# Value products of two head pairs in one group, up products grouped by operand, first loads by single row blocks, last update in unequal pieces

## The chip, the cores and the metric

The kernel runs on one core of one Trainium2 chip. A core has a matrix engine (TensorE, "PE" in the profile, with its weight loads under "PEld"), VectorE (DVE), ScalarE (ACT), GpSimd (POOL, all but unused here) and SyncE (SP), whose queue issues every transfer of this kernel. PE reads its operands from on-chip memory (SBUF) and writes into an accumulator memory (PSUM); ACT and DVE carry results out of it. The metric is the time of one execution in device microseconds, and the median over runs is compared.

## The reference, cut to what matters

Two layers of a decoder over 256 tokens of width 1024, in float32. Each layer has eight heads of sparse attention (three branches: compressed, selected, window), eight heads of forgetting attention, an output projection, and a squared-ReLU MLP, each wrapped in norms:

```python
for l in range(DEPTH):                       # DEPTH = 2
    h = _rms_norm(x, g_pre_mix[l])
    parts = jnp.split(h @ w_in[l], split_at, axis=-1)      # 1024 -> 2848 columns
    ...
    o_nsa = _nsa_mixer(...)                  # 8 heads of 64, branches gated by a sigmoid
    o_fox = _fox_mixer(...)                  # 8 heads of 64, decayed causal softmax
    mix = jnp.concatenate([o_nsa, o_fox], axis=-1) @ w_out[l]
    x = x + _rms_norm(mix, g_post_mix[l])
    h = _rms_norm(x, g_pre_mlp[l])
    y = jnp.square(jax.nn.relu(h @ w_up[l])) @ w_down[l]   # 1024 -> 4096 -> 1024
    x = x + _rms_norm(y, g_post_mlp[l])
```

With 256 tokens, selection keeps all four blocks and the window reaches over all tokens, so the selected and the window branch are both causal softmax attention over the whole sequence, each with its own keys and values.

## The kernel before, in words

**Arithmetic.** A float32 product is made of three products in a faster float32 form: each operand is split into a high part (an ACT copy, `whi` for weights) and a low remainder (a DVE subtraction, `wlo`), and the three products high-high, high-low and low-high are summed in PSUM (`mm3`). So each weight unit passes three steps: a transfer from memory into a raw buffer (`wraw`, four buffers, `RBUFS`), the ACT copy, and the DVE subtraction, after which the raw buffer is free. Attention probabilities, transposes and value products are plain float32.

**Order.** Nothing is issued in the order of the program text. A recorder (`Recorder`) collects all operations, then plays them through a planner with assumed costs and due times (`order`, line 243) and writes out one fixed order per engine. Each engine then runs its list in order, waiting on semaphores where operands are late. A `stretch` (line 182) binds several PE products into one piece of the plan; the planner charges 145 ns (`RETILE`) when the shape of the PE array that a product uses changes.

**Start.** `FIRSTS` (line 41) cuts the first 512-column chunk of the input projection by row blocks of 128: units of 1, 1, 2, 2 and 2 blocks. Lines 537 to 546 issue, on SP, the head (gains and row block 0 of x transposed), then weight units and blocks of x transposed (`xt`) in turns. Behind them come x itself in four pieces, constants, and the units of the next chunk. For the first units the split is done block by block (line 442).

**Attention.** Steps run over a flat list: for the sparse heads, pairs 0 to 3, two heads a pair, branches 1 and 2; then the forgetting heads, pairs 0 to 3, two heads. A step computes scores; one step later the probabilities are scaled; two steps later `probs_T` (line 1141) transposes them on PE (three transposes of 128x128) and copies them to SBUF as `prT`; three steps later, when a pair is complete, `pv` (line 1152) makes the value products of the pair in a stretch: 64-column weights, the two heads side by side, 8 products for a sparse pair and 4 for a forgetting pair, each run in two passes. A sparse pair adds one 128-column product with `vbig` for the compressed branch. `o_evac` (line 1167) splits the 256 columns of the result into high and low parts (`oT`). Between these steps PE is filled with products of the input projection and later of the output projection (`fill`). PSUM holds one accumulator of the kind "o".

**Output projection, MLP.** `out_last` (line 1283) finishes the output projection with blocks 4 to 7, which need the forgetting heads. In `up` (line 1319) the transposed up projection has weights stationary and tokens moving: for each of 28 column blocks of 128 a layer, and each of eight row blocks, one product of the high weights with 512 moving columns (high and low tokens side by side) and one of the low weights with 256. `down` products have 512 moving columns.

**End.** `sandwich` (line 656) applies the last norm and adds the result into x, in halves of 512 columns for each of the two token tiles, and stores each half.

Of the kernel before, what the change touches and what calls it, by code (L numbers as in the profile page):

```python
# [18 lines left out]
F32 = mybir.dt.float32  # L19
F32R = mybir.dt.float32r  # L20
AF = mybir.ActivationFunctionType
OP = mybir.AluOpType
PSUM = bass.MemoryType.PSUM

P = 128
# [12 lines left out]
RETILE = 145  # L38
SEQ = [(2, 0), (2, 1), (2, 2), (2, 3), (3, 0), (3, 1), (3, 2), (3, 3)]
EVKEY = 1  # L40
FIRSTS = [(0, 1), (1, 2), (2, 4), (4, 6), (6, 8)]
UPK = 7
TOK, WBUFS, RBUFS = 6, 7, 4
LOAD_LEAD, SPLIT_LEAD, RIDE_LEAD = 12, 1, 6
# [366 lines left out]
class Weights:  # L411
# [12 lines left out]
    def get(self, i):  # L424
        nc, marks = self.nc, self.marks
        assert len(marks) == i
        marks.append(len(nc.ops))
        if i not in self.raw:
            nc.key = marks[max(i - LOAD_LEAD, 0)]
            if self.units[i][0] == "raw":  # L430
                nc.after = nc.ops[marks[max(i - RIDE_LEAD, 0)] - 1]
            self.load(i)
            nc.after = None
        kind, shape, src = self.units[i]
        raw = self.raw.pop(i)
        nc.key = None
        if kind == "raw":
            return raw
        nc.key = marks[max(i - SPLIT_LEAD, 0)]
        hi = self.tile([P] + shape, F32R, name="whi", tag="whi", bufs=WBUFS)  # L440
        lo = self.tile([P] + shape, F32R, name="wlo", tag="wlo", bufs=WBUFS)
        for j in range(shape[0]) if i < len(FIRSTS) else [slice(None)]:
            nc.scalar.activation(hi[:, j], raw[:, j], AF.Copy)
            nc.vector.tensor_sub(lo[:, j], raw[:, j], hi[:, j].bitcast(F32))
        nc.key = None
        return hi, lo
# [14 lines left out]
def trunk(nc, A, consts_in, out, sbp, pp):  # L461
# [75 lines left out]

    nc.sync.dma_start(head, A["xT"][:, 0:8 + S])
    W.load(0)
    load_xt(1, 3)  # L540
    W.load(1)
    W.load(2)
    load_xt(3, 5)
    W.load(3)
    load_xt(5, 8)
    W.load(4)
    nc.after = nc.ops[-1]

    def load_rest():
# [106 lines left out]
    def sandwich(t, acc, g_post, pre=None, xT=None, r4=None, r2=None, store=None):  # L656


        sq = small([P, 2], "sq")
        m, mg = [None, None], [None, None]  # L660

        def times(name, n, gain):
            y = tokt(name)
            if r2 is None:
                nc.vector.tensor_mul(y, acc[n], gain[:, half(n)])
            else:
                nc.vector.scalar_tensor_tensor(y, acc[n], r2, gain[:, half(n)], op0=OP.mult, op1=OP.mult)
            return y

        for n in range(2):  # L670
            junk = small([P, 512], "rl")
            nc.scalar.activation(junk, acc[n], AF.Square, scale=1.0 / 32.0, accum_out=sq[:, n:n + 1])
            if pre:
                mg[n] = times("mg", n, pre[0])
            if n == 0 and not pre:
                m[0] = times("m", 0, g_post)
        r = rsqrt_sum(sq[:, 0:1], sq[:, 1:2], r4)
        if not pre:
            m[1] = times("m", 1, g_post)
        if pre:  # L680
            xg = []
            for n in range(2):
                xg.append(mg[n])
                for c in (0, 256):
                    a = n * 512 + c
                    nc.vector.scalar_tensor_tensor(xg[n][:, c:c + 256], mg[n][:, c:c + 256], r,
                                                   pre[1][t][:, a:a + 256], op0=OP.mult, op1=OP.add)
            yield
            for n in range(2):
                to_xT(t, n, xg[n], xT)  # L690
            yield
        for n in range(2):
            if pre:
                m[n] = times("m", n, g_post)
            nc.vector.scalar_tensor_tensor(X[t][:, half(n)], m[n], r, X[t][:, half(n)],
                                           op0=OP.mult, op1=OP.add)
            if store is not None:
                nc.sync.dma_start(store[:, half(n)], X[t][:, half(n)])
        yield

    def rope(dst, src, t, nh):
# [28 lines left out]
    for l in range(DEPTH):  # L730
# [407 lines left out]
                    nc.vector.tensor_scalar(p[:, a:b], p[:, a:b], st[:, 2 + t:3 + t], gate[t][:, c:c + 1],  # L1138
                                            op0=OP.mult, op1=OP.mult)

        def probs_T(p, eng):
            ps = psum("s")
            for a in (0, 128, 256):
                nc.tensor.transpose(ps[:, a:a + P], p[:, a:a + P], ident)
            pT = small([P, 384], "prT", 6)
            if eng:
                nc.scalar.activation(pT, ps[:, :384], AF.Copy)
            else:
                nc.vector.tensor_copy(pT, ps[:, :384])
            return pT  # L1150

        def pv(o, terms, last):

            with nc.stretch():
                for i, (pT, V, cols) in enumerate(terms):
                    for kb in range(2):
                        for par in range(2):
                            h = slice(par * HD, par * HD + HD)
                            c = cols[par]
                            if kb == 0:  # L1160
                                nc.tensor.matmul(o[h, 0:S], V[0][:, c:c + HD], pT[par][:, 0:S],
                                                 start=i == 0, stop=False, skip_group_check=True)
                            else:
                                nc.tensor.matmul(o[h, P:S], V[1][:, c:c + HD], pT[par][:, S:S + P],
                                                 start=False, stop=last and i == len(terms) - 1, skip_group_check=True)

        def o_evac(o, kind, pair):
            if (kind, 0) not in oT:
                for j in range(2):
                    oT[kind, j] = tile([P, 4, S], F32R, name="oT", tag=f"act{j}", bufs=2)  # L1170
            split(o[:, :S], [oT[kind, j][:, pair, :] for j in range(2)])
            done.add(("o", pair + (0 if kind == "nsa" else 4)))


        if first:
# [70 lines left out]
        for i in range(len(flat) + 4):  # L1246
            if 0 <= i - 1 < len(flat):
                scale(flat[i - 1], *st[i - 1])
            if i < len(flat):
                st[i] = scores(flat[i])  # L1250
                if i == 15:
                    done.add("nsa")
                    g_post, g_pre2 = load_gains(("g_post_mix", l), ("g_pre_mlp", l))
            fill(1)
            if i in side:
                side[i]()
                fill(1)
            if 0 <= i - 2 < len(flat):
                pTs[flat[i - 2]] = probs_T(st.pop(i - 2)[0], i % 2)
            fill(1)  # L1260
            j = i - 3
            if 0 <= j < len(flat) and flat[j][2] == 1 and flat[j][3] != 1:
                kind, pair, par, br = flat[j]
                o = psum("o")
                cols = [(pair // 2) * HD] * 2 if br else [2 * pair * HD, 2 * pair * HD + HD]
                pv(o, [([pTs.pop((kind, pair, x, b)) for x in range(2)], (fV, vS, vW)[b], cols)
                       for b in ((1, 2) if br else (0,))], not br)
                if br:
                    nc.tensor.matmul(o[:, :S], T["vbig"][:, pair].rearrange("p j d -> p (j d)"), T["pcT"],
                                     start=False, stop=True, skip_group_check=True)  # L1270
                o_evac(o, kind, pair)
            if i >= 12 or i % 2:
                fill(1)

# [44 lines left out]
        def up(fc, then=None):  # L1319
            a = [tile([P, 4, S], F32R, name="aT", tag=f"act{j}", bufs=2) for j in range(2)]  # L1320
            for b in range(4):
                hi, lo = weight(l, "up", fc, b)

                ps = psum("s")
                for k in range(8):
                    nc.tensor.matmul(ps, hi[:, k, :], xT[2][:, k].rearrange("p j n -> p (j n)"), start=k == 0, stop=False,
                                     skip_group_check=True)
                    nc.tensor.matmul(ps[:, S:], lo[:, k, :], xT[0][:, k, :], start=False, stop=k == 7,
                                     skip_group_check=True)
                if then is not None and b == 1:  # L1330
                    then()
                if b % 2 == 0:
                    h = tokt("h")
                d = h[:, (b % 2) * S:(b % 2) * S + S]
                nc.scalar.activation(d, ps[:, S:], AF.Copy)
                nc.vector.tensor_add(d, ps[:, :S], d)
                if b % 2:
                    rl = small([P, 512], "rl")
                    nc.scalar.activation(rl, h, AF.Relu)
                    nc.vector.tensor_mul(h, rl, rl)  # L1340
                    d = [y[:, b - 1:b + 1, :].rearrange("p b n -> p (b n)") for y in a]
                    nc.scalar.activation(d[0], rl, AF.Square)
                    nc.vector.tensor_sub(d[1], h, d[0].bitcast(F32))
# [122 lines left out]
```

## Time and profile before

| what | value |
|---|---|
| median of 3 runs | 635.33 us (635.32 to 635.46) |
| the profiled execution | 635.77 us, span 634.0 us |
| PE busy | 625.5 us, 99% of the span |
| ACT, DVE busy | 373.8 us, 480.9 us |
| DMA | 115.75 MB, mean 183 GB/s |

A row of a timeline gives start, duration, engine, line (L350 is the one line through which the recorder emits everything), operation, output and inputs by tile name, the array shape, the output's shape, and a count where rows are merged. Matmuls are pipelined, so a row's duration overlaps the next; what one costs is the distance between starts. A float32 product that isn't a transpose appears as two instructions, its two passes.

### The profile page before, as it was taken

The page shows a single profiled execution, that of the slowest core. Times are in us where ns is not written, and L with a number is a line of the kernel's source. Part 1 is how long each engine was busy: PE and PEld are TensorE (multiplying, and loading weights), DVE is VectorE, ACT ScalarE, POOL GpSimd, SP SyncE. Part 2 cuts the span into 40 slices and gives each one's busy share as a digit, 9 for nine tenths or more (in the row PEclk, how much of TensorE's full clock was granted, in tenths as well). Part 3 has the DMA queues.
Part 4 walks back from the last instruction along what each step waited for, and adds up shares of the span by engine and source line. Part 5 has one row for each costly group of instructions (what it writes and reads, how often), then busy time and mean ns, then how long its engine had stood idle before and what let it go on. Part 6 is the DMA issues. An engine that isn't in the chain of part 4 may idle for free.

```text
span 634.0 us, 9913 instructions
## 1 busy us (share of the span) xinstructions
PE 625.5 (99%) x3570; PEld 520.4 (82%) x3570; DVE 480.9 (76%) x1084; ACT 373.8 (59%) x737; POOL 0.2 (0%) x4
## 2 busy tenths in 40 slices
PE   9999999999999999999999999999999999999995
PEld 6888977688888888888888988777888888888884
DVE  6899998869985665566598999987998665666544
ACT  7865676564864455456467656864658464455432
POOL 0000000000000000000000000000000000000000
PEclk9999999999999999999999999999999999999999
DMA  8998436225786666656329954432267766655601
GB/s 307 345 321 284 131 100 168 85 67 174 247 280 196 196 178 197 194 185 183 121 81 308 331 167 130 166 101 67 66 230 259 228 184 197 197 184 186 197 1 66
DMA packets 47005, 115.75 MB, mean 183 GB/s; under 512 B 4003, under 2 KB 14573, under 8 KB 46957
## 3 DMA queue, kind: packets, MB, share of 16 engines
q1 hardware_dynamic: 46956, 115.13, 56.8%
q8 instruction: 28, 0.46, 0.3%
q14 instruction: 21, 0.16, 0.1%
HBM read 114.07 MB, written 1.05 MB: 182 GB/s over the span
## 4 chain that ended last, share of the span: by engine, by line
PE 98%; DMA 1%; DVE 0%; ACT 0%; SPq 0%; issue 0%; DVEq 0%
PE s L350 35%; PE acc L350 31%; PE x L350 25%; PE o L350 7%; DMA wraw<-in_w_in_dram 1%; SPq L350 0%; DVE x L350 0%; DVE m L350 0%; DVEq L1462 0%; ACT whi L350 0%; ACT xT L350 0%; DVE rsqrt L350 0%; ACT rl L350 0%; DVEq L350 0%
## 5 line engine op out<-in xcount | busy, mean ns | idle before, releaser
L350 DVE TENSOR_TENSOR wlo<-wraw,whi 128x1024 fp32r<-128x1024 f32 (+2 forms) x196 | 230.2, 1180 | 101.8 <-ACT whi L350 100.1
L350 ACT ACTIVATE whi<-wraw 128x1024 fp32r<-128x1024 f32 (+2 forms) x196 | 199.7, 1025 | 157.0 <-PE acc L350 74.2
L350 PE MATMUL s<-xT,whi 128*128 128x512 f32 x448 | 158.5, 397 | 0.0
L350 PE MATMUL s<-xT,wlo 128*128 128x256 f32 x448 | 125.7, 281 | 0.0
L350 PEld LDWEIGHTS s<-xT,whi 128*128 128x128 f32 x448 | 84.1, 188 | 20.5
L350 PE MATMUL acc<-whi,aT 128*128 128x512 f32 x256 | 88.9, 391 | 0.0
L350 PE MATMUL x<-whi,aT 128*128 128x512 f32 x256 | 88.8, 391 | 0.0
L350 PEld LDWEIGHTS s<-xT,wlo 128*128 128x128 f32 x448 | 84.6, 189 | 0.6
L350 PEld LDWEIGHTS x<-whi,aT 128*128 128x128 f32 x256 | 47.9, 188 | 10.2
L350 PEld LDWEIGHTS acc<-whi,aT 128*128 128x128 f32 x256 | 48.0, 188 | 10.0
L350 ACT ACTIVATE pr<-pr,st 128x128 f32<-128x128 f32 (+1 forms) x96 | 42.8, 447 | 17.5 <-DVE st L350 17.1
L350 PE MATMUL acc<-wlo,aT 128*128 128x512 f32 x128 | 49.9, 390 | 0.0
L350 PE MATMUL x<-wlo,aT 128*128 128x512 f32 x128 | 49.9, 390 | 0.0
L350 PE MATMUL acc<-xT,whi 128*128 128x256 f32 x256 | 49.4, 285 | 0.0
L350 PEld LDWEIGHTS acc<-xT,whi 128*128 128x128 f32 x256 | 40.4, 190 | 2.3 <-issue 1.4
L350 PE MATMUL x<-whi,xT 128*128 128x512 f32 x112 | 37.9, 408 | 0.5 <-ACT whi L350 0.3
L350 PE MATMUL acc<-whi,xT 128*128 128x512 f32 (+1 forms) x128 | 38.2, 359 | 0.0
L350 PE MATMUL acc<-xT,wlo 128*128 128x256 f32 x128 | 36.3, 286 | 0.0
L350 ACT ACTIVATE rl<-x 128x512 f32<-128x512 f32 x24 | 14.7, 612 | 24.9 <-PE x L350 16.8
L350 PEld LDWEIGHTS acc<-wlo,aT 128*128 128x128 f32 x128 | 24.0, 188 | 5.1
L350 PEld LDWEIGHTS x<-wlo,aT 128*128 128x128 f32 x128 | 24.0, 188 | 4.6
L350 ACT ACTIVATE h<-s 128x256 f32<-128x256 f32 x56 | 20.6, 368 | 10.7 <-PE s L350 10.7
(219 smaller groups left out, 963.2 us busy)
## 6 DMA issues: line engine op xcount, KB each, us to landing
wraw<-in_w_up_dram SPq DMA_DIRECT2D x64, 512.0 KB, 3.7
wraw<-in_w_down_dram SPq DMA_DIRECT2D x64, 512.0 KB, 3.9
wraw<-in_w_in_dram SPq DMA_DIRECT2D x39, 512.0 KB, 5.0
wraw<-in_w_out_dram SPq DMA_DIRECT2D x16, 512.0 KB, 3.6
w<-in_cmp_w_k_dram SPq DMA_DIRECT2D x8, 512.0 KB, 5.4
w<-in_cmp_w_v_dram SPq DMA_DIRECT2D x8, 512.0 KB, 8.2
wraw<-in_w_in_dram SPq DMA_DIRECT2D x8, 288.0 KB, 5.1
x<-in_x_dram SPq DMA_DIRECT2D x4, 256.0 KB, 7.4
```

What stands on the lines that cost most here:

```text
L350: getattr(getattr(self.nc, op.engine), name)(*[real(v) for v in args], **{k: real(v) for k, v in kw.items()})
```

## The change

Four edits, independent of each other in the code:

- **Value products.** `pv` now takes two pairs and makes their products in one stretch, into the two halves of one 512-column accumulator; it is called when the odd pair is complete. The two `vbig` products follow together, and `o_evac` splits 512 columns at once. The transposed probabilities of the even pair must live until then, so those of odd sparse pairs go into a buffer `prX`, taken from the two-buffer rings `act0` and `act1` that also hold `oT` and the MLP's activations.
- **Up products.** In `up` the eight products with the high weights come first, then the eight with the low weights.
- **First loads.** `FIRSTS` has seven units (1, 1, 1, 1, 1, 1 and 2 blocks), and the blocks of x transposed come as 1, 1, 1, 2 and 2. The high part of the very first unit is copied half by ACT and half by DVE.
- **Last update.** With a store, the second half of x (512 columns) is updated and stored in pieces of 320 and 192.

```diff
-FIRSTS = [(0, 1), (1, 2), (2, 4), (4, 6), (6, 8)]
+FIRSTS = [(0, 1), (1, 2), (2, 3), (3, 4), (4, 5), (5, 6), (6, 8)]
...
-            nc.scalar.activation(hi[:, j], raw[:, j], AF.Copy)
+            if i == 0:
+                h = shape[1] // 2
+                nc.scalar.activation(hi[:, j, :h], raw[:, j, :h], AF.Copy)
+                nc.vector.tensor_copy(hi[:, j, h:], raw[:, j, h:])
+            else:
+                nc.scalar.activation(hi[:, j], raw[:, j], AF.Copy)
...
     W.load(0)
-    load_xt(1, 3)
-    W.load(1)
-    W.load(2)
-    load_xt(3, 5)
-    W.load(3)
-    load_xt(5, 8)
-    W.load(4)
+    for i, (a, b) in enumerate(FIRSTS[1:], 1):
+        if a != 5:
+            load_xt(a, max(b, 6) if a == 4 else b)
+        W.load(i)
...
-            nc.vector.scalar_tensor_tensor(X[t][:, half(n)], m[n], r, X[t][:, half(n)],
-                                           op0=OP.mult, op1=OP.add)
-            if store is not None:
-                nc.sync.dma_start(store[:, half(n)], X[t][:, half(n)])
+            for a, b in ((0, 320), (320, 512)) if store is not None and n else ((0, 512),):
+                c = slice(n * 512 + a, n * 512 + b)
+                nc.vector.scalar_tensor_tensor(X[t][:, c], m[n][:, a:b], r, X[t][:, c], op0=OP.mult, op1=OP.add)
+                if store is not None:
+                    nc.sync.dma_start(store[:, c], X[t][:, c])
...
-            pT = small([P, 384], "prT", 6)
+            kind, pair, par, br = e
+            if kind == "nsa" and pair % 2:
+                if br == 1:
+                    T["prX"] = tile([P, 4, S], F32, name="prX", tag=f"act{par}", bufs=2).rearrange("p b n -> p (b n)")
+                pT = T["prX"][:, (br - 1) * 384:br * 384]
+            else:
+                pT = small([P, 384], "prT", 6)
...
-        def pv(o, terms, last):
+        def pv(o, pairs, last):
             with nc.stretch():
+                for q, terms in enumerate(pairs):
...
+                                    nc.tensor.matmul(o[h, q * S:q * S + S], V[0][:, c:c + HD], pT[par][:, 0:S],
+                                                     start=q == 0 and i == 0, stop=False, skip_group_check=True)
...
-            split(o[:, :S], [oT[kind, j][:, pair, :] for j in range(2)])
+            split(o.rearrange("p (b n) -> p b n", b=2), [oT[kind, j][:, pair - 1:pair + 1, :] for j in range(2)])
...
                 for k in range(8):
                     nc.tensor.matmul(ps, hi[:, k, :], xT[2][:, k].rearrange("p j n -> p (j n)"), start=k == 0, stop=False,
                                      skip_group_check=True)
+                for k in range(8):
                     nc.tensor.matmul(ps[:, S:], lo[:, k, :], xT[0][:, k, :], start=False, stop=k == 7,
                                      skip_group_check=True)
```

More of the change, by code (lines that the diff above doesn't have):

```diff
@@ L1139, in scale, with probs_T @@
                                             op0=OP.mult, op1=OP.mult)
-        def probs_T(p, eng):
+        def probs_T(p, eng, e):
             ps = psum("s")
@@ L1150, in probs_T @@
             return pT
-        def pv(o, terms, last):
+        def pv(o, pairs, last):
             with nc.stretch():
[L1155 to L1165, printed above, removed]
+                for q, terms in enumerate(pairs):
+                    for i, (pT, V, cols) in enumerate(terms):
+                        for kb in range(2):
+                            for par in range(2):
+                                h = slice(par * HD, par * HD + HD)
+                                c = cols[par]
+                                if kb == 0:
+                                    nc.tensor.matmul(o[h, q * S:q * S + S], V[0][:, c:c + HD], pT[par][:, 0:S],
+                                                     start=q == 0 and i == 0, stop=False, skip_group_check=True)
+                                else:
+                                    nc.tensor.matmul(o[h, q * S + P:q * S + S], V[1][:, c:c + HD], pT[par][:, S:S + P],
+                                                     start=False, stop=last and i == len(terms) - 1,
+                                                     skip_group_check=True)
         def o_evac(o, kind, pair):
@@ L1170, in o_evac @@
                     oT[kind, j] = tile([P, 4, S], F32R, name="oT", tag=f"act{j}", bufs=2)
-            split(o[:, :S], [oT[kind, j][:, pair, :] for j in range(2)])
-            done.add(("o", pair + (0 if kind == "nsa" else 4)))
+            split(o.rearrange("p (b n) -> p b n", b=2), [oT[kind, j][:, pair - 1:pair + 1, :] for j in range(2)])
+            for x in (pair - 1, pair):
+                done.add(("o", x + (0 if kind == "nsa" else 4)))
         if first:
@@ L1258, in trunk @@
             if 0 <= i - 2 < len(flat):
-                pTs[flat[i - 2]] = probs_T(st.pop(i - 2)[0], i % 2)
+                pTs[flat[i - 2]] = probs_T(st.pop(i - 2)[0], i % 2, flat[i - 2])
             fill(1)
@@ L1263, in trunk @@
                 kind, pair, par, br = flat[j]
[L1264 to L1271, printed above, removed]
+                if pair % 2:
+                    o = psum("o")
+                    cols = lambda q: [(q // 2) * HD] * 2 if br else [2 * q * HD, 2 * q * HD + HD]
+                    pv(o, [[([pTs.pop((kind, q, x, b)) for x in range(2)], (fV, vS, vW)[b], cols(q))
+                            for b in ((1, 2) if br else (0,))] for q in (pair - 1, pair)], not br)
+                    if br:
+                        for q in range(2):
+                            nc.tensor.matmul(o[:, q * S:q * S + S], T["vbig"][:, pair - 1 + q].rearrange("p j d -> p (j d)"),
+                                             T["pcT"], start=False, stop=True, skip_group_check=True)
+                    o_evac(o, kind, pair)
             if i >= 12 or i % 2:
```

## The prediction

> **What bounds the kernel now.** I read the page first: span, busy shares, and the chain that ended last.
>
> ```profile
> span 634.0 us, 9913 instructions
> PE 625.5 (99%) x3570; PEld 520.4 (82%) x3570; DVE 480.9 (76%) x1084; ACT 373.8 (59%) x737; POOL 0.2 (0%) x4
> PE 98%; DMA 1%; DVE 0%; ACT 0%; SPq 0%; issue 0%; DVEq 0%
> ```
>
> PE is 99% busy and 98% of the chain. A busy PE could still be one that waits, so next came the waits with PE as the waiting engine, whole list, and stretches of the span (columns: length, then busy time and count of PE, PEld, DVE, ACT, POOL, then clock, DMA share, GB/s).
>
> ```profile
> PE o L350 <- DVE warm L350: 1.2, 1, 1.2
> PE x L350 <- ACT whi L350: 0.3, 1, 0.3
> PE x L350 <- ACT xT L350: 0.2, 1, 0.2
> ```
>
> ```profile
> 0.00:18.00 18.00, 16.50 (x59) 12.49 (x60) 10.70 (x30) 13.57 (x32) 0.20 (x4) 1.00 0.90 307
> 18.00:52.00 34.00, 33.97 (x249) 29.94 (x248) 30.39 (x83) 23.21 (x42) 0.00 (x0) 1.00 1.01 339
> 52.00:127.00 75.00, 75.00 (x534) 59.22 (x533) 68.57 (x240) 49.16 (x141) 0.00 (x0) 1.00 0.46 140
> ```
>
> Between 18 us and the last product PE hardly waits for anybody. So the time is the start of 18 us, plus a fixed list of PE instructions at the distance each needs from the next, plus the tail. Removing work from ACT or DVE gives nothing; changing distances in PE's list gives all of it. The number of products is the same before and after (3,334 products and transposes, counted in the written-out order); only their neighbours change.
>
> **Up products: -2.3 us.** First the chain in order of time (start, length, what), then PE's timeline in an up stretch and in a stretch where 256-column products follow each other.
>
> ```profile
> 194.35 11.29 PE s L350 x64
> ...
> 621.72 5.45 PE acc L350 x24
> ```
>
> ```profile
> 194.19 0.39 PE L350 MATMUL s<-xT,whi 128*128 128x512 f32 x1
> 194.41 0.28 PE L350 MATMUL s<-xT,wlo 128*128 128x256 f32 x1
> 194.53 0.40 PE L350 MATMUL s<-xT,whi 128*128 128x512 f32 x1
> ```
>
> ```profile
> 51.38 0.40 PE L350 MATMUL acc<-xT,whi 128*128 128x256 f32 x2
> 51.62 0.28 PE L350 MATMUL acc<-xT,wlo 128*128 128x256 f32 x1
> ...
> 52.82 0.40 PE L350 MATMUL acc<-xT,whi 128*128 128x256 f32 x2
> ```
>
> 64 products, four column blocks, take 11.29 us: 2.82 us a block, 0.353 us for a pair of 512 and 256 columns. In a run of 512s (`acc`, 24 in 5.45 us) one takes 0.227; in a run of 256s (12 starts between 51.38 and 52.82) one takes 0.120. Together 0.347. Grouped, a block is 8 x 0.227 + 8 x 0.120 = 2.78 us, 0.04 less; over 28 blocks in each of 2 layers, 56 x 0.0415 = 2.3 us. The written-out order shows runs of exactly eight and eight. Bounds: 0 (the distances don't depend on the neighbour) and 56 x 0.0865 = 4.8 us (a low product in a run at 0.115, the lower edge of the rounded 0.12 between 194.41 and 194.53). The run of 256s is the nearest row, so I take 2.3. ACT's read of the block waits for the last low product as before, and high and low weights of a unit are both there before their block starts.
>
> Here a rule speaks against the edit. The Trainium skill, "TensorE: Matmul & The Clock Gate", section "Back-to-back issue gap", gives the warm distance of isolated products as columns/2.4 ns plus 2.5 ns, without regard to the neighbour: an estimate of 215.8 + 109.2 = 325 ns a pair in either order, and nothing to gain. By it the sum below would be short of the whole 2.3. The trace has 353 ns for the pair and 347 for the two runs, so the distances here are longer than the rule's and do depend on the order.
>
> **Value products: -2.4 us.** PE's timeline around a forgetting pair (eight instructions) and a sparse pair (two rows of eight):
>
> ```profile
> 121.67 0.62 PE L350 MATMUL acc<-whi,oT 128*128 128x512 f32 x2
> 122.22 0.87 PE L350 MATMUL o<-prT,fV 128*64 128x256 f32 x8
> 123.02 0.50 PE L350 MATMUL acc<-wlo,oT 128*128 128x512 f32 x1
> 123.36 0.27 PE L350 MATMUL s<-cst,pr 128*128 128x128 f32 x1
> ```
>
> ```profile
> 91.91 0.87 PE L350 MATMUL o<-prT,vS 128*64 128x256 f32 x8
> 92.61 0.82 PE L350 MATMUL o<-prT,vW 128*64 128x256 f32 x8
> 93.36 0.55 PE L350 MATMUL s<-cst,pr 128*128 128x128 f32 x3
> ```
>
> Eight instructions occupy 122.22 to 123.02, 0.80 us; sixteen 91.91 to 93.36, 1.45. So eight more cost 0.65 and each visit 0.15 besides. Its edges cost too: from 121.67 to 123.36 pass 1.69 us, of which three 512-column products are 0.68 and the streaming 0.65; 0.36 is left for one visit. The change has 8 visits in place of 16. Bounds: 8 x 0.15 = 1.2 and 8 x 0.36 = 2.9; I take 0.30 a visit, nearer the upper row, since some visits begin or end at float32 transposes, where the edge is already paid: 2.4 us. The two `vbig` products that now follow each other I leave at 0 (bounds 0 and -0.4: one of their passes is shorter when it follows its like). Visits to the transposes are 92 before and 91 after, so that toll stays.
>
> What the grouping delays: the even pair's result appears one pair later, and the split reads 512 columns. The last group of a layer on PE, the two rows of its split, and ACT's for 512 columns from PSUM:
>
> ```profile
> 125.74 0.87 PE L350 MATMUL o<-prT,fV 128*64 128x256 f32 x8
> 126.66 0.39 ACT L350 ACTIVATE oT<-o 128x256 fp32r<-128x256 f32 x1 [1.31 <-PE o L350]
> 127.08 0.42 DVE L350 TENSOR_TENSOR oT<-o,oT 128x256 fp32r<-128x256 f32 x1 [0.85 <-ACT oT L350]
> 130.95 0.60 ACT L350 ACTIVATE rl<-x 128x512 f32<-128x512 f32 x1 [2.03 <-PE x L350]
> ```
>
> The group's 0.80 us end at 126.54 and ACT begins 0.12 later; with 512 columns the high half would be there 0.12 + 0.60 = 0.7 us after the group, the low half another 0.7 later (0.42 grown with the columns). The new order puts five output products (1.1 us) between that group and the first that needs the high half. That covers it: 0. Without that cover the low half would set the end, 1.4 us after the group and needed two products (0.45) after the high one: 1.0 us a layer. The other groups have scores, transposes and output products behind them, over 2 us. `prX` stands in the rings `act0` and `act1`: its first buffer is free since the previous MLP, and it is freed by the group before the forgetting heads' `oT` asks for one; 0.
>
> **First loads: 0.** The start up to the second chunk, ACT, DVE and PE:
>
> ```profile
> 8.32 1.15 ACT L350 ACTIVATE whi<-wraw 128x512 fp32r<-128x512 f32 x2 [0.66 <-DMA wraw<-in_w_in_dram]
> ...
> 12.67 1.15 ACT L350 ACTIVATE whi<-wraw 128x512 fp32r<-128x512 f32 x2
> 16.85 0.67 ACT L350 ACTIVATE whi<-wraw 128x576 fp32r<-128x576 f32 x1
> 17.55 0.76 DVE L350 TENSOR_TENSOR wlo<-wraw,whi 128x576 fp32r<-128x576 f32 x1 [0.52 <-ACT whi L350]
> 18.37 0.40 PE L350 MATMUL acc<-wlo,xT 128*128 128x288 f32 x1
> ```
>
> Smaller pieces let row block 1 begin some 0.4 us sooner (0.13 MB less stands ahead of its weights, at 307 GB/s), and the shared first copy gives 0.1. But PE then meets the second chunk, whose low weights are done at 17.55 + 0.76 = 18.31; PE takes them at 18.37 already. ACT comes to that chunk when the last unit of the first one (12.67) and the squares of x are through, and those hang on transfers: the same bytes, with the transfer engines 0.90 busy. So what is gained ahead is waited for at 18.3.
>
> The change also makes SP wait. With four raw buffers, the fifth, sixth and seventh unit wait for the low split of the first three, and behind them on SP's queue stand x, constants and the next chunk; PE waits for those at 18.3. Per unit of `wraw` in this stretch:
>
> ```profile
> DMA to landing us min/median/max: 4.1/5.7/7.3
> ```
>
> The third unit, for which ACT now waits until 8.32, has half its bytes and lands near 7.5; with a block's copy (0.6) and subtraction (0.7) it frees its buffer near 9.0. Issued then, the seventh lands at 13.1 with the shortest landing shown and at 14.7 with the median, against 12.67 now: +0.4 to +2.0 if the wait counts fully, down to -0.4 if the gained start survives. But of the 2.6 MB issued before it (head, six units, x transposed) only 2.1 have moved by 9.0, at 307 GB/s since 2 us; half a megabyte, 1.6 us of transfer, is still ahead, and hides most of the wait. I take 0.
>
> **Last update: -0.1 us.** DVE and SP at the end:
>
> ```profile
> 629.40 1.42 DVE L350 SCALAR_TENSOR_TENSOR x<-m,rsqrt,x 128x512 f32<-128x512 f32 x2
> 630.18 0.99 SPq L350 DMA_DIRECT2D out_dram<-x  x2
> out_dram<-x SPq DMA_DIRECT2D x4, 256.0 KB, 2.0
> ```
>
> Two updates take 1.42; the second ends at 630.82 and its store starts at 630.84, 2.0 us to landing. Two pieces cost one instruction more, about 0.1, and a third issue (0.33) that must follow the second: the last store starts near 631.0, 0.16 later, but carries 96 KB, not 256. At 339 GB/s that is 0.48 us less if nothing stands ahead of it, and nothing less if the same 512 KB leave in one stream. Between -0.3 and +0.2 I take -0.1.
>
> **Sum.** -2.3 - 2.4 + 0 - 0.1 = -4.8. The profiled execution took 635.77 us, 1.8 more than its span and 0.44 more than the median of 635.33. So 631.0 for an execution like it, and 630.5 for the median.
>
> **Rivals.**
> 1. The grouping of up products does nothing, and a pair costs 0.353 in any order: 635.3 - 2.5 = 632.8. Against it stand the two runs above; for it, that the run of 256s is taken from a stretch where two of three products share their weights. The rule named above would give this time.
> 2. Late value groups: at the end of both layers' attention PE waits for the split of 512 columns, 1.0 us each, since behind it come the output products and the norm: 630.5 + 2.0 = 632.5. For it: twice the columns in one piece, and one accumulator of this kind. Against: 0.7 against 1.1 us of cover, and before, PE waits nowhere in such places.
> 3. Slower: the waits of SP at the start run the transfer queue dry. Three units in turn wait for a split and each lands 4.1 us or more after issue; if nothing overlaps, the start grows by up to 8 us, 635.3 - 4.8 + 8 = 638.5. It decides from 4.8 + 1.3 = 6.1 us of delay at 18.3. Against: the half megabyte still queued when the last of them is issued.
>
> **How the numbers follow.** Chances: forecast 0.71 (630.5, own range 629.4 to 632), rival 1 0.12, rival 2 0.09, rival 3 0.08. 0.2% is about what a measurement of this kernel can tell from no change, 1.3 us. Lower end: value products at 2.9, start at 0.4, tail at 0.3 and up as forecast, 5.9 in all, give 629.4; more than that, from the far bound of the up products, I hold under 1 in 10. Upper end: the first two rivals (632.8, 632.5), 633.0. Faster 0.88; within 0.2% 0.05 (a start late by 3.5 to 6.1 us); slower 0.07.
>
> **What would show it.** Right: 64 up products in about 11.12 us; 1.45 us for 16 forgetting instructions in one row; PE's waits still under 1 us in sum after 20 us; the low split of the second chunk ending at 18.3 within 0.3. Wrong: up still at 11.29; PE waiting for `oT` near the end of attention; ACT waiting for transfers between 9 and 13 us; the second chunk starting past 19 us; products spread so that visits to the transposes pay more than now.

## The result and the profile after

The changed kernel takes 632.48 us (median of 4 runs, 632.41 to 632.73) against 635.39 us before (4 runs, 635.32 to 635.72): a ratio of 0.9954 with a 95% interval of 0.994 to 0.9968. It is faster by 2.9 us where 4.8 us were forecast. The sign held, and so did the outer range (629.4 to 633.0); the forecast's own range (629.4 to 632) and its size didn't, and the experiments below say which term took the 1.9 us.

The profiled execution took 632.41 us. Its page gives span, busy time and count of instructions, and the chain that ended last by engine:

```profile
span 630.4 us, 9929 instructions
PE 620.3 (98%) x3570; PEld 520.7 (83%) x3570; DVE 481.5 (76%) x1079; ACT 372.9 (59%) x729; POOL 0.2 (0%) x4
PE 95%; DVE 2%; DMA 1%; ACT 0%; issue 0%; SPq 0%; DVEq 0%
```

PE lost 5.2 us of busy time (625.5 before), yet the span only shrank by 3.6 us, and PE's share of the chain fell from 98% to 95%. So PE now waits more. The list of waits with PE as the waiting engine (us in total, times, longest) had three entries before; now it has seven:

```profile
PE o L350 <- DVE warm L350: 1.2, 1, 1.2
PE x L350 <- ACT whi L350: 0.7, 1, 0.7
PE acc L350 <- DVE fkT L350: 0.4, 1, 0.4
PE s L350 <- DVE rsqrt L350: 0.3, 1, 0.3
PE acc L350 <- DVE wlo L350: 0.3, 1, 0.3
PE x L350 <- DVE wlo L350: 0.2, 1, 0.2
PE x L350 <- ACT xT L350: 0.2, 1, 0.2
```

Those on `warm` and `xT` are as before; all the others but the one on `fkT` lie in the first 20 us. PE's timeline there (start, duration, engine, line, operation, tiles, shapes, and in brackets the idle time with what ended it):

```profile
18.52 0.49 PE L350 MATMUL s<-cst,rsqrt 128*128 128x128 f32 x2 [0.28 <-DVE rsqrt L350]
19.00 0.53 PE L350 MATMUL acc<-whi,xT 128*128 128x288 f32 x2
19.79 0.40 PE L350 MATMUL acc<-wlo,xT 128*128 128x288 f32 x1 [0.26 <-DVE wlo L350]
```

The first product with low weights of the second chunk starts at 19.79, where it started at 18.37: 1.42 us late. The last product of the kernel, before and then after:

```profile
626.77 0.39 PE L350 MATMUL acc<-whi,aT 128*128 128x512 f32 x1
```

```profile
623.25 0.39 PE L350 MATMUL acc<-whi,aT 128*128 128x512 f32 x1
```

Between these two products the changed order takes 603.46 us (19.79 to 623.25) against 608.40 before (18.37 to 626.77): 4.94 us less. But 0.46 us of this belongs to the one profiled execution of the kernel before and not to the change: the kernel with the up grouping alone (below) has the same list of PE products up to 149 us, and its products between 18.4 and 60 us take 0.46 us less. That leaves 4.5 us, where 4.7 were forecast for the two groupings. **The steady part gained nearly what was forecast; the start took 1.4 us of it back.**

What is late at the start? ACT's rows in the same trace show it idle for 2 us ahead of the last unit of the first chunk, which it took at 12.67 before:

```profile
10.82 1.14 ACT L350 ACTIVATE whi<-wraw 128x512 fp32r<-128x512 f32 x2
13.99 1.15 ACT L350 ACTIVATE whi<-wraw 128x512 fp32r<-128x512 f32 x2 [2.03 <-DMA wraw<-in_w_in_dram]
```

SP's queue before, and then after (start and duration of the stretch in which the transfers of a row are issued):

```profile
5.34 0.38 SPq L350 DMA_DIRECT2D wraw<-in_w_in_dram  x1
5.76 2.88 SPq L350 DMA_DIRECT2D x<-in_x_dram  x4
```

```profile
5.50 3.78 SPq L350 DMA_DIRECT2D wraw<-in_w_in_dram  x3
9.33 0.46 SPq L350 DMA_DIRECT2D x<-in_x_dram  x1
```

Before, the last unit of the first chunk is issued at 5.34 and x right behind it. After, three units are spread over 5.50 to 9.28, although one issue takes 0.3 to 0.5 us: SP waits in between for raw buffers, and x starts at 9.33 instead of 5.76. In the stretch from 9 to 14 us (length; busy time and count of PE, PEld, DVE, ACT, POOL; clock, DMA share, GB/s), first before, then after:

```profile
9.00:14.00 5.00, 5.00 (x23) 4.10 (x22) 5.00 (x10) 4.93 (x11) 0.00 (x0) 1.00 1.05 396
```

```profile
9.00:14.00 5.00, 5.00 (x23) 3.88 (x22) 3.76 (x8) 2.95 (x8) 0.00 (x0) 1.00 0.88 287
```

The transfers run at 287 GB/s in place of 396. Over 5 us that is 0.545 MB less, or 1.4 us at 396 GB/s, which agrees with the 1.42 us by which the second chunk is late. What the second chunk hangs on is the landing of that last unit: at 12.65 before, at 13.97 after. In all twelve traces of this document the first low product of the second chunk starts 5.71 to 5.82 us after it.

The two groupings, in rows of the changed kernel. An up stretch, from PE's timeline and from the chain (start, length, what):

```profile
193.48 1.98 PE L350 MATMUL s<-xT,whi 128*128 128x512 f32 x8
195.29 1.11 PE L350 MATMUL s<-xT,wlo 128*128 128x256 f32 x8
196.24 2.00 PE L350 MATMUL s<-xT,whi 128*128 128x512 f32 x8
198.08 1.12 PE L350 MATMUL s<-xT,wlo 128*128 128x256 f32 x8
```

```profile
193.64 11.15 PE s L350 x64
```

Eight 512-column products take 1.81 to 1.84 us (0.226 to 0.230 each), eight of 256 columns 0.95 (0.119 each). The 64 products take 11.15 us, where they took 11.29; 11.12 was forecast.

The value products of a forgetting group (16 instructions) and of a sparse group (32):

```profile
124.77 1.52 PE L350 MATMUL o<-prT,fV 128*64 128x256 f32 x16
126.22 0.50 PE L350 MATMUL x<-wlo,oT 128*128 128x512 f32 x1
```

```profile
86.71 0.87 PE L350 MATMUL o<-prT,vS 128*64 128x256 f32 x8
87.41 0.82 PE L350 MATMUL o<-prT,vW 128*64 128x256 f32 x8
88.06 0.82 PE L350 MATMUL o<-prX,vS 128*64 128x256 f32 x8
88.71 0.82 PE L350 MATMUL o<-prX,vW 128*64 128x256 f32 x8
89.46 0.44 PE L350 MATMUL s<-cst,pr 128*128 128x128 f32 x2
```

Sixteen take 1.45 us and 32 take 2.75, so a pair costs 0.65 and each doubling saves the 0.15 inside, as worked out; the edges come on top.

The one new wait behind the start is in the second layer, where PE goes from the transposed chunk of keys to the next chunk. PE before, then PE after, then DVE before and DVE after:

```profile
385.26 0.40 PE L350 MATMUL acc<-xT,whi 128*128 128x256 f32 x2
385.59 0.87 PE L350 MATMUL o<-prT,vS 128*64 128x256 f32 x8
386.29 0.82 PE L350 MATMUL o<-prT,vW 128*64 128x256 f32 x8
387.50 0.28 PE L350 MATMUL acc<-xT,wlo 128*128 128x256 f32 x1
387.62 0.40 PE L350 MATMUL acc<-whi,xT 128*128 128x512 f32 x1
```

```profile
384.28 0.28 PE L350 MATMUL acc<-xT,wlo 128*128 128x256 f32 x1
385.00 0.50 PE L350 MATMUL acc<-whi,xT 128*128 128x512 f32 x1 [0.44 <-DVE fkT L350]
```

```profile
385.85 0.68 DVE L350 TENSOR_TENSOR fkT<-acc,rT 128x512 f32<-128x512 f32 x1
```

```profile
383.14 1.21 DVE L350 TENSOR_TENSOR wlo<-wraw,whi 128x1024 fp32r<-128x1024 f32 x1
384.26 1.28 DVE L350 TENSOR_TENSOR fkT<-acc,rT 128x512 f32<-128x512 f32 x2
```

The keys fill two accumulators. Before, a sparse pair's value products (1.4 us) stood between the last product into the first accumulator (385.14) and the last ones into the second (to 387.50). DVE carried out the first one behind that cover, at 385.85, and the next chunk's product followed after 0.12 us. In the new order no value products stand there, DVE comes to the first accumulator at 384.26, behind a low split, and the next chunk's product waits 0.6 us (from 384.28 to 385.00, less the 0.12 of a 256-column product). The first layer has the same place with a distance of 0.35 us, a stall of 0.23; there the kernel before already has a distance of 0.24, so only half of that stall is new.

### The profile page after: what moved, and what is told of

It reads as the page before. It is cut to its first block, busy times and chain, and to the rows that moved or that the text cites. A ratio compares the mean times of both kernels' runs of the same rounds, so it can differ in the third digit from the quotient of the medians.

```text
span 630.4 us, 9929 instructions
## 1 busy us (share of the span) xinstructions
PE 620.3 (98%) x3570; PEld 520.7 (83%) x3570; DVE 481.5 (76%) x1079; ACT 372.9 (59%) x729; POOL 0.2 (0%) x4
## 3 DMA queue, kind: packets, MB, share of 16 engines
HBM read 114.07 MB, written 1.05 MB: 183 GB/s over the span
## 4 chain that ended last, share of the span: by engine, by line
PE 95%; DVE 2%; DMA 1%; ACT 0%; issue 0%; SPq 0%; DVEq 0%
PE s L350 35%; PE acc L350 30%; PE x L350 23%; PE o L350 7%; DMA wraw<-in_w_in_dram 1%; DVE wlo L350 0%; ACT whi L350 0%; DVE pr L350 0%; DVE fkT L350 0%; SPq L350 0%; DVE x L350 0%; DVE m L350 0%; ACT xT L350 0%; DVE rsqrt L350 0%; DVE prT L350 0%
## 5 line engine op out<-in xcount | busy, mean ns | idle before, releaser
L350 ACT ACTIVATE whi<-wraw 128x1024 fp32r<-128x1024 f32 (+3 forms) x196 | 199.5, 1023 | 134.1 <-PE acc L350 67.9
L350 PE MATMUL s<-xT,whi 128*128 128x512 f32 x448 | 112.0, 392 | 0.0
L350 PEld LDWEIGHTS s<-xT,whi 128*128 128x128 f32 x448 | 81.4, 189 | 15.2
L350 PEld LDWEIGHTS s<-xT,wlo 128*128 128x128 f32 x448 | 61.1, 190 | 4.4
L350 PE MATMUL s<-xT,wlo 128*128 128x256 f32 x448 | 62.5, 282 | 0.0
L350 PE MATMUL acc<-whi,xT 128*128 128x512 f32 (+1 forms) x128 | 36.2, 355 | 0.5 <-DVE fkT L350 0.4
L350 ACT ACTIVATE rl<-x 128x512 f32<-128x512 f32 x24 | 14.7, 612 | 24.9 <-PE x L350 16.7
```

The costliest lines, as they stand in the source:

```text
L350: getattr(getattr(self.nc, op.engine), name)(*[real(v) for v in args], **{k: real(v) for k, v in kw.items()})
```

## The experiments

Ratios are to the kernel before, measured beside each set: 635.63 us for the first four, 635.68 for the next four, 635.66 for the last two.

### The up grouping alone

```diff
                     nc.tensor.matmul(ps, hi[:, k, :], ...
+                for k in range(8):
                     nc.tensor.matmul(ps[:, S:], lo[:, k, :], ...
```

> Before with the up products grouped, nothing else. Theory: 64 up products in 11.12 us in place of 11.29, 2.3 us in all: 633.1. Rival: the distances belong to the products and not to their neighbours: 11.29 us and 635.4.

Measured: 633.23 us (633.17 to 633.36), ratio 0.996 (0.9947 to 0.9972), 2.40 us less. In its trace the up stage is 1.06 us shorter in either layer (143.79 in place of 144.85), 2.1 in both; the other 0.3 of the medians lies inside the interval (1.8 to 3.4). The order of the products does matter, and rival 1 falls. The Trainium skill, "TensorE: Matmul & The Clock Gate", section "Back-to-back issue gap", has no such dependence in its formula for isolated products, by which 0 would have been left; here the measurement decides.

### The value grouping alone

```diff
-            pT = small([P, 384], "prT", 6)
+            ... prX in the rings act0 and act1 for odd sparse pairs
-        def pv(o, terms, last):
+        def pv(o, pairs, last):
...
+                if pair % 2:
```

> Before with the value products of two pairs in one group, nothing else. Theory of the prediction: 8 visits fewer at 0.30 us, 633.0. Rival, from the trace after: 8 visits fewer give 2.4, but PE meets new waits where the accumulators of the fifth chunk are released late by DVE (0.2 us in the first layer, 0.6 in the second), 633.8.

Measured: 633.31 us (633.01 to 633.46), ratio 0.996 (0.9948 to 0.9973), 2.32 us less. The trace has the gain unevenly: beside the up grouping alone, which has the old value products, the time from the first product of the compression (`o<-w,kstk`) to the up stage is 1.49 us shorter in layer 1 and 0.87 in layer 2. PE's waits include the one on `fkT` (0.5 us), so 2.3 is what is left after it.

### Everything but the first loads

```diff
-FIRSTS = [(0, 1), (1, 2), (2, 3), (3, 4), (4, 5), (5, 6), (6, 8)]
+FIRSTS = [(0, 1), (1, 2), (2, 4), (4, 6), (6, 8)]
...
-    for i, (a, b) in enumerate(FIRSTS[1:], 1):
...
+    load_xt(1, 3)
+    W.load(1)
...
```

with the shared first copy taken out too.

> The changed kernel with the first loads of before (units of 1, 1, 2, 2, 2 blocks, x transposed in three transfers, first copy on ACT alone). Theory: the finer first loads cost the 1.42 us by which the second chunk's first low-weight product came later (18.37 before, 19.79 after). Then it stands at 18.4 again and the time is 632.48 - 1.4 = 631.1 us. Rival: the transfers bound the kernel up to 52 us anyway, and the delay would have been lost there in part: the delay was 1.42 at 19.8 us and 1.19 at 50 us, so a gain of at most 1.2, 631.3 or more. Second rival: the first loads gained 0.1 to 0.4 in their own chunk and the loss has another cause (buffers held by the grouped value products): then no gain, 632.5.

Measured: 630.69 us (630.54 to 631.78), ratio 0.9924 (0.9911 to 0.9938). That is 4.9 us less than before, the forecast for the whole change, and 1.8 us less than the change with its first loads, 0.4 more than the delay of 1.42 us explains, and that lies inside the interval. PE meets the second chunk as it did before the change:

```profile
17.70 0.51 PE L350 MATMUL acc<-whi,xT 128*128 128x288 f32 x2
18.30 0.40 PE L350 MATMUL acc<-wlo,xT 128*128 128x288 f32 x1
```

### The new first loads, without SP's waits for raw buffers

The changed kernel, but units 4 to 6 get buffers of their own (in rings that are free at the start), so that none waits for a low split.

```diff
-                       self.tile([P] + shape, F32, name="wraw", tag="raw", bufs=RBUFS))
+                       self.tile([P] + shape, F32, name="wraw", tag=f"act{i % 2}" if 4 <= i < 7 else "raw",
+                                 bufs=2 if 4 <= i < 7 else RBUFS))
```

> The changed kernel, but the fifth, sixth and seventh weight unit land in buffers of the rings act0 and act1, which stand empty then, so that SP waits for no low split among the first loads. Theory: SP's wait for raw buffers makes the loss at the start. Then the seventh unit lands at 12.7 us or before (13.97 with the wait), the second chunk's first low-weight product comes at 18.4 or before, and the time is 631.1. Rival: the pieces themselves cost it (more transfers with fewer bytes each, eight in flight at most): the unit still lands near 14.0, the product stays at 19.8 and the time at 632.5.

Measured: 631.08 us (631.03 to 631.47), ratio 0.9927 (0.9915 to 0.994). 1.4 of the 1.8 us come back. SP's queue, and the stretch from 9 to 14 us:

```profile
6.78 0.38 SPq L350 DMA_DIRECT2D wraw<-in_w_in_dram  x1
7.49 2.53 SPq L350 DMA_DIRECT2D x<-in_x_dram  x4
```

```profile
9.00:14.00 5.00, 5.00 (x22) 4.00 (x23) 4.17 (x9) 4.28 (x9) 0.00 (x0) 1.00 1.04 396
```

The pieces are as small as in the changed kernel and come in the same number; only the wait for buffers is gone. The last unit is issued 2.1 us sooner (6.78 against 8.90), x 1.8 us sooner, and the transfers run at 396 GB/s again. So it is the waits of SP, not the smaller pieces, that thin out the transfers. The unit lands at 13.06 and not at 12.7 as expected, and the first low product of the second chunk starts at 18.77, still 0.4 later than before. That is no more than executions with the old loads differ by (landings from 12.52 to 13.06, products from 18.23 to 18.78 in nine of them), and the 0.39 us between this kernel and the last one lies inside both intervals: whether small pieces cost anything by themselves stays open.

### The new first loads alone

```diff
-FIRSTS = [(0, 1), (1, 2), (2, 4), (4, 6), (6, 8)]
+FIRSTS = [(0, 1), (1, 2), (2, 3), (3, 4), (4, 5), (5, 6), (6, 8)]
...
+                nc.vector.tensor_copy(hi[:, j, h:], raw[:, j, h:])
```

> The kernel before with the new first loads alone (seven units, blocks of x transposed in turn, first copy shared). If SP's waits for raw buffers are the cause of the missing time, and the parts add up, this is slower than before by the 1.8 us that the changed kernel has over the one with the old loads: 637.4 us (636.9 to 637.9), with the first low product of the second chunk near 19.8 us instead of 18.4. If the prediction's term was right (0) and the loss comes only from the parts together, it is 635.6 us and that product stays at 18.4.

Measured: 637.02 us (636.54 to 637.95), ratio 1.0024 (1.0014 to 1.0035): slower by 1.3 us, with 0.9 to 2.2 inside the interval. The loss is there without any grouping, at the same place:

```profile
19.70 0.40 PE L350 MATMUL acc<-wlo,xT 128*128 128x288 f32 x1 [0.26 <-DVE wlo L350]
```

The expected 637.4 was a little high; 1.3 alone and 1.8 beside the groupings are not told apart by the intervals.

### Without the unequal last update

The groupings with the old loads and the old last update.

```diff
-            for a, b in ((0, 320), (320, 512)) if store is not None and n else ((0, 512),):
...
+            nc.vector.scalar_tensor_tensor(X[t][:, half(n)], m[n], r, X[t][:, half(n)],
+                                           op0=OP.mult, op1=OP.add)
```

> Up and value grouping only; first loads and last update as before. Beside the 630.7 us of the kernel that has the unequal last update as well, the prediction's term of -0.1 gives 630.8; its bounds give 631.0 (-0.3) and 630.5 (+0.2). From the last product to the end of the span I expect 7.2 us, against 7.17 with unequal pieces. A difference under 0.3 us between the two medians can't be told from none here; the trace's tail decides.

Measured: 631.17 us (630.99 to 631.35), ratio 0.9929 (0.9917 to 0.9942), against 630.69 with it (another set) and 630.99 with it and the shared copy (the same set). The tail can't be the whole of that: from the start of the last product to the end of the span pass 7.21 to 7.22 us here and in five other traces with the old last update, and 7.14 to 7.18 in the five with the new one, 0.06 less. But a seventh with the old update, the one with the new first loads alone, has 6.93, and no run says why. So a gain of some 0.05 us is likely, below what the medians can tell: the term is not confirmed, and not refuted.

### The shared first copy

The groupings, the unequal last update and the old loads, with the very first copy shared.

```diff
+            if i == 0:
+                h = shape[1] // 2
+                nc.scalar.activation(hi[:, j, :h], raw[:, j, :h], AF.Copy)
+                nc.vector.tensor_copy(hi[:, j, h:], raw[:, j, h:])
```

> The kernel with grouped up and value products, the loads of before and the unequal last update, and in addition the very first copy shared by ACT and DVE. The prediction said that what is gained ahead is waited for at 18.3 us: then 630.7 us, no change, the first product about 0.1 us sooner and the first low product of the second chunk at 18.3 as before. If the start were bound by the first copy, everything behind would move by the 0.1 us: 630.6.

Measured: 630.99 us (630.54 to 631.45), ratio 0.9926 (0.9913 to 0.9938), against 630.69 without it in the first set. The first product starts at 4.55 in place of 4.63, the first low product of the second chunk at 18.59 in place of 18.30. The gain ahead is not to be found behind: no change that can be measured.

### The wait for fkT taken away

The kernel without the first loads; the last weight part of the transposed chunks is worked off accumulator by accumulator, so that the first one is complete sooner and DVE can carry it out while PE fills the second. The products are the same.

```diff
-                for k in range(k0, k1):
-                    for b in range(4):
+                seq = ([(k, b) for k in range(k0, k1) for b in range(4)] if k1 < 8 else
+                       [(k, b) for a in (0, 2) for k in range(k0, k1) for b in (a, a + 1)])
+                for k, b in seq:
```

> The same kernel with the loads of before, and the last weight part of the transposed chunks taken accumulator by accumulator, so that the first of the two accumulators is complete half a part (about 1.5 us of PE) sooner. If the new wait of PE on DVE's eviction of fkT in the second layer (0.45 us in the list of waits, about 0.5 of lost distance) is a cost that the value grouping's order brought, and the first accumulator is all that the next chunk needs at first, it goes: 630.2 us. If PE then waits for the second accumulator instead, or another wait takes its place, 630.7 as without the edit.

Measured: 630.01 us (629.54 to 630.54), ratio 0.9911 (0.9898 to 0.9925), 1.0 to 1.2 us less than the two kernels of the same set that have both groupings without the edit; the kernel that it was made from, in another set, has 630.69, 0.7 more. From the second chunk's first low product to the last product, 602.57 us pass here and 603.47 there. Its waits of PE, and the place in question:

```profile
PE o L350 <- DVE warm L350: 1.2, 1, 1.2
PE x L350 <- ACT whi L350: 1.0, 1, 1.0
PE x L350 <- ACT xT L350: 0.2, 1, 0.2
```

```profile
382.81 0.28 PE L350 MATMUL acc<-xT,wlo 128*128 128x256 f32 x1
382.93 0.40 PE L350 MATMUL acc<-whi,xT 128*128 128x512 f32 x1
```

The next chunk's product follows after 0.12 us, and both stalls (0.23 and 0.61 us in the kernel it was made from) are gone. **This version is the best of all: 5.7 us less than before, and 2.5 less than the change as made.**

### The same edit on the kernel before, and with the value grouping alone

The same diff in both.

> The kernel before with only the reordered last weight part of the transposed chunks. The kernel before shows no wait of PE for fkT, so if the edit's gain in the changed order is the removed wait, nothing is to be had here: 635.6 us (635.2 to 636.0; the written-out order shifts elsewhere too). If the edit is a gain by itself, whatever the value products do (better distances in those chunks), it gives the same 0.9 us here: 634.7.

Measured: 635.47 us (635.1 to 635.8), ratio 0.9992 (0.9984 to 1.0001). In the kernel before, whose list of waits has none on `fkT`, the edit does nothing that can be measured.

> The kernel before with the value grouping and the reordered last weight part. The value grouping alone measured 633.31 us against 635.63, and its trace has two stalls of PE at the change from the transposed chunk to the next one, 0.23 us in layer 1 and 0.62 in layer 2. If these are a cost of the grouping, and the grouping itself is worth 2.3 + 0.85 = 3.2 us, this gives 632.4 us, with no wait of PE for fkT. If the edit only moves a wait, 633.3.

Measured: 632.44 us (632.2 to 633.01), ratio 0.9947 (0.9935 to 0.9959), 3.22 us less than before and 0.87 less than the value grouping without the edit; PE's list of waits has no `fkT`. So the wait is a cost of the value grouping, and the grouping itself is worth 3.2 us by the medians, with 2.6 to 4.1 inside the interval. By the traces it is less: with the edit in both, the time from the first product of the compression to the up stage falls from 109.89 to 108.29 us in layer 1 and from 109.84 to 108.73 in layer 2, 2.7 us in all.

## Why the prediction was right in sign and wrong in size

| term | forecast | measured | from |
|---|---|---|---|
| up products | -2.3 | -2.40 | the up grouping alone |
| value products | -2.4 | -2.32 | the value grouping alone |
| of it: 8 visits fewer | -2.4 | -2.7 to -3.2 | with the `fkT` wait removed, by traces and by medians |
| of it: what is late next | 0 | +0.6 to +0.9 | the stalls in the traces, and the edit that removes them |
| first loads | 0 | +1.3 to +1.8 | alone, and by leaving them out |
| last update | -0.1 | not resolved | tails of twelve traces |
| sum | -4.8 | -2.9 | the change |

- **PE's list sets the time.** Right, for all that lies behind the start. The two groupings alone give 2.40 and 2.32 us, and together, with the last update, 4.9.
- **Up products.** Right in mechanism, and its size in part by luck. 0.14 us a stretch of 64 products, over 14 such stretches, is 2.0 by the chain's rows; 2.1 by the two stages of the trace. The prediction's own rows give more than the 2.3 that it wrote: 2.8225 less 8 x (0.227 + 0.120) is 0.046 us a block and not 0.0415, so 2.6 us.
- **Value products.** The sum came out right because two errors cancel, which is luck. The toll of a visit was taken as 0.30 us, with 0.36 as the upper bound; 2.7 to 3.2 us over 8 visits are 0.34 to 0.40, near that bound or above it. Some of it may be the two `vbig` products that now follow each other (0 to 0.4 us, left at 0); no run parts the two. The other error is what the grouping delays. The prediction followed the delayed *result* and found it covered, and it was: ACT's split of 512 columns begins 0.12 us after the group and takes 0.60, DVE's 0.69, and no wait of PE for `oT` shows. It didn't follow the delayed *group* itself, which had been the cover of an eviction that has nothing to do with values.

```profile
126.34 0.60 ACT L350 ACTIVATE oT<-o 128x512 fp32r<-128x512 f32 x1 [1.97 <-PE o L350]
```

- **First loads: the step that failed.** The prediction worked out that the last unit, issued near 9.0, would land between 13.1 and 14.7 us against 12.67, "+0.4 to +2.0 if the wait counts fully". It was issued at 8.90 and landed 5.07 us later, at 13.97. Then it took 0 on the ground that half a megabyte was still queued and "hides most of the wait". It hid none: +1.3 us at the last unit became +1.42 at the second chunk. What was queued did not keep the rate up. When the last unit was issued, four transfers were in flight; before, SP kept eight in flight at that time, and each of its issues from 8.3 us on starts right after a landing. From 10 to 15 us the changed kernel moved 219 to 299 GB/s (in steps of 1 us), the kernel before 359 to 416. The experiment with buffers of its own shows that SP's waits bring this about: same pieces, no such wait, 396 GB/s. Why the rate stays low until 15 us, although eight transfers are in flight again from 12.6 as far as landings are recorded, no run shows.
- **The range.** 632.48 us is outside the forecast's own range and close to the times of rivals 1 and 2 (632.8 and 632.5), which set the upper end of the outer one. Both were refuted; that the outer range held is luck, owed to a third cause of like size.
- **Rivals.** Rival 1 fell with the up grouping alone. Rival 2 didn't appear. Rival 3, SP's waits at the start, is the mechanism that acted, at 1.4 us in the trace and not from 6.1 upwards. Two signs that the prediction named as wrong came: ACT waits for a transfer from 12 to 14 us, and the second chunk starts at 19.00, its first low product at 19.79. Of the signs named as right, the low split of the second chunk ends at 19.74 and not at 18.3; the other three came (11.15 us for 64 up products, 1.45 for 16 instructions of a forgetting group, 0.6 us of waits after 20 us).
- **Last update.** DVE takes three instructions in 1.54 us, where two took 1.42: the 0.12 of the forecast. Its three last stores start within 1.3 us, and the span ends 3.8 us after the first of these issues. The sum of it, 0.04 us in this trace, is lost in the scatter.

```profile
625.88 1.54 DVE L350 SCALAR_TENSOR_TENSOR x<-m,rsqrt,x 128x512 f32<-128x512 f32 x3
626.66 1.30 SPq L350 DMA_DIRECT2D out_dram<-x  x3
```

## What to carry to other kernels

When a transfer is cut into more pieces than there are buffers, the issuing queue waits for compute, and everything queued behind it starts late; count what must have landed by the next fixed point, not whether the transfer engines are still busy. When a group of products moves, ask what it covered where it stood, besides asking who waits for its result. And test the parts of a change one by one: here two of four parts made the gain, one took a third of it back, and a wait of 0.6 to 0.9 us that the gain itself had brought could be removed by reordering the products of one weight part.

## What the runs showed of the hardware that was not expected

- **A pause of the issuing queue costs rate, and the busy share hardly shows it.** With the transfer engines still 0.88 busy in the records, 287 GB/s were moved, and 396 at 1.05. In the first 18 us of the changed kernel the times from issue to landing per weight unit are:

```profile
DMA to landing us min/median/max: 2.7/4.8/6.2
```

  The shortest is 2.7 us for 256 KB. The Trainium skill, "DMA: Bandwidth & Descriptors", section "Anatomy of one DMA", gives a fixed 2.0 us and the bytes at 436 GB/s, fitted on transfers that GpSimd issues. For 256 KB that makes an estimate of 2.6 us, and the trace, with SP issuing, agrees.
- **Changing the shape of the array costs 0.34 to 0.40 us a visit**, worked out from 2.7 to 3.2 us over 8 visits fewer, of which only 0.15 us lie inside the visit's own rows. The Trainium skill, "TensorEngine Tiling (Array Packing)", section "Key Properties", says that a change of the tiling mode drains TensorE and gives no price. The traces show a cost at the edges of a visit, as the rule would have it; that it is a drain, no run shows.
- **The start differs between executions by 0.5 us with the same loads** (first low product of the second chunk at 18.23 to 18.78 in nine traces of kernels with the old loads), while the steady part repeats better: from there to the last product, the five kernels with both groupings and without the edit for `fkT` take 603.4 to 603.7 us.
